# A transformer block pair on one Trainium2 core: order of work between the last attention step and the second MLP

## The chip, the cores and the metric

The kernel runs on one core of a Trainium2 chip. A core has a matrix engine (PE; its weight loads are listed apart as PEld), a vector engine (DVE), a scalar engine (ACT), a general engine (POOL) and a queue engine that issues transfers (SP). The engines run side by side and meet through semaphores. Matrix products land in PSUM, eight banks of 128 by 512 floats; everything else lies in on-chip SBUF or in HBM. The metric is the device time of the whole program in microseconds.

## The reference

The reference runs two layers over 256 latent tokens and 256 context tokens of width 1024. Layer 0 mixes by retention, layer 1 by neighbourhood attention with 32 heads; a squared-ReLU MLP of hidden width 4096 follows each. Six modulation vectors a layer come from a small product with `ada_w`. Only the latent tokens are returned, so layer 1 needs its MLP for 256 tokens alone. What matters here is the end of layer 1:

```python
x = layer_norm(DN_ALPHA * x + g1 * y, ln_g[i, 0], ln_b[i, 0])     # y = attention output @ nat_w_o
h = x * (1.0 + sc2) + sh2
x = layer_norm(DN_ALPHA * x + g2 * sq_relu_mlp(h, mlp_w1[i], mlp_w2[i]), ln_g[i, 1], ln_b[i, 1])

def sq_relu_mlp(h, w1, w2):
    return jnp.square(jax.nn.relu(h @ w1)) @ w2
```

All of it is float32. The kernel gets that from a faster format by splitting each operand into a high part, rounded to `float32r`, and a low part, the rest. A product is then three: high by high, high by low, low by high.

## The kernel before

**Weights.** `specs` lists all weight blocks in the order of use, each 512 KB. `fetch(n)` takes the next n: SP loads the block into one of four `raw` buffers, ACT casts it to a `hi` tile, and the subtraction that makes the `lo` tile is put on the list `pending`. `lows(n)` has DVE do the next n of that list. `take(n, ahead, open_)` hands out n blocks; first it fetches and subtracts until `ahead` blocks (five, where nothing is said) are there from its first on. There are five `hi` and five `lo` tiles. A `raw` buffer is free again once its low part is made, so SP's next load into it waits for DVE. With `at=` a block goes to a named slot (`hilo`), with `in_scratch` into small scratch tiles.

**Order.** Each engine has a queue that it works through in order. The wrappers `pe`, `act`, `dve` and `pool` have a switch `on`: while it is on, the engine keeps the order in which the program is written; while it is off, a scheduler chooses. In all that the change touches, the switch is on for PE, ACT and DVE (for POOL from line 1902 on); lines 2062 and 2063 turn it off inside the first feature block of the second MLP. SP always keeps the written order. So the written order is the order in each queue, and an instruction that waits holds back all behind it.

**The last attention step** (lines 1851 to 1872). Attention runs over 16 steps n. `scores(n)` multiplies queries and keys, `soften(n)` adds the bias and takes the exponential, `invert(n)` takes the reciprocal of the sums on DVE (and copies it to `rr`), `gather(n)` copies a corner of each result on POOL, `flip(n)` turns the results on PE (`ppt`) and copies them out (`pt`; the tiles j = 1 and 3 on DVE, the others on ACT), then turns `rr` into the bank `av`. `turned(n)` copies that to `rt`. `attend(n)` multiplies by the values, scales by `rt` on DVE and splits into `oTh` and `oTl`. Between them stand `fetch` and `lows` for the output weights.

**Output projection and norm** (lines 1874 to 2005). `mmo` multiplies `oTh` and `oTl` by output weights. `settle_last` and `settle_quarter` gate the result, add it to the residual `R`, and take statistics; `moments` ends with a power on POOL (`rstd`); `center` writes the normalised `xn`, half on DVE, half on ACT. `mod_pt` turns `xn` on PE, and `affine_half` (lines 1933 to 1939, token block 0) or `direct` (token block 1) scales, shifts and splits it into `hTh` and `hTl`.

**First feature block** (lines 2006 to 2048). Token blocks 0 and 1 become ready one after the other, so the first 512 features are done by tokens: `tok_part` multiplies one token block's `hTh` or `hTl` by a weight unit's high or low part. `p00`, `p01`, `p10` and `p11` are the banks for token block 0 or 1 and feature half 0 or 1 (all named `p1t` in the profile). HH is high by high, HL tokens high by weight low, LH tokens low by weight high. `activate` squares the ReLU on ACT and DVE (`r`), and `turn_block` turns the square on PE (`pt`) and splits it into `hid` on ACT and DVE.

**The other features** (lines 2054 to 2070). Seven blocks of two calls follow, by features: `mm1` does 48 products of 256 tokens into two banks `p`, and `relu_sq` squares and splits each. Then come the products with `mlp_w2`, gate, norm and output.

Of the kernel before, what the change touches and what calls it, by code (L numbers as in the profile page):

```python
# [10 lines left out]
F32 = mybir.dt.float32  # L11
# [98 lines left out]
def kernel(  # L110
# [23 lines left out]
    pe, act, dve, pool, sp = (  # L134
        InOrder(tc, getattr(nc, e), e in PIN)
        for e in ("tensor", "scalar", "vector", "gpsimd", "sync")
    )
# [19 lines left out]
    def nm(s):  # L157
        uid[0] += 1
        return f"{s}_{uid[0]}"
# [4 lines left out]
    def slot(i, shape, dt, s):  # L164

        return arena.tile(shape, dt, tag=f"s{i}", name=nm(s))

    def scr(s, dt=F32):
        return scp.tile([P, 512], dt, tag="scr", name=nm(s))
# [90 lines left out]
    def fetch(n, in_scratch=False, at=None):  # L260

        for src, k, ncol in specs[len(units) : len(units) + max(n, 0)]:
            raw = rawp.tile([P, k, ncol], F32, tag="raw", name=nm("raw"))
            sp.dma_start(out=raw[:], in_=src.rearrange("(k p) n -> p k n", p=P))
            if in_scratch or len(units) in scratch_units:
                hi, lo = Rows([scr("hi", F32R) for _ in range(k)]), Rows([scr("lo", F32R) for _ in range(k)])
                for i in range(k):
                    act.copy(out=hi[:, i, :], in_=raw[:, i, :])
                    pending.append((lo[:, i, :], raw[:, i, :], hi[:, i, :]))
                units.append((hi, lo))  # L270
                continue
            if at is None:
                hi = hip.tile([P, k, ncol], F32R, tag="hi", name=nm("hi"))
                lo = lop.tile([P, k, ncol], F32R, tag="lo", name=nm("lo"))
            else:
                both = slot(at, [P, 2, k, ncol], F32R, "hilo")
                hi, lo = both[:, 0], both[:, 1]
            act.copy(out=hi[:], in_=raw[:])
            pending.append((lo[:], raw[:], hi[:]))
            units.append((hi, lo))  # L280

    def lows(n=100):
        for lo, raw, hi in pending[:n]:
            dve.tensor_sub(out=lo, in0=raw, in1=hi.bitcast(F32))
        del pending[:n]

    def take(n, ahead=WB, open_=0):
        first = taken[0]
        while len(units) < min(first + max(n, ahead), len(specs)):
            fetch(1)  # L290
            lows()
        taken[0] = first + n
        assert len(units) - len(pending) >= first + n - open_
        return units[first : first + n]
# [312 lines left out]
    def mod_aff(pt, half, t, A, B, on_act=None, halves=False):  # L607

        tmp = scr("aff")
        for i in range(4):  # L610
            k = 4 * half + i
            a, b = A[:, k, t // 2 : t // 2 + 1], B[:, k, t // 2 : t // 2 + 1]
            o, x_ = tmp[:, tsl(i)], pt[:, tsl(i)]
            if halves:
                o = o.rearrange("p (b r c) -> p b r c", b=2, r=2)
                x_ = x_.rearrange("p (r b c) -> p b r c", b=2, r=2)
            if not (half if on_act is None else on_act):
                dve.tensor_scalar(out=o, in0=x_, scalar1=a, scalar2=b, op0=ALU.mult, op1=ALU.add)
            else:
                act.activation(out=o, in_=x_, func=AF.Identity, scale=a, bias=b)  # L620
        return tmp
# [40 lines left out]
    def rstd_of(mv, eng=pool):  # L662
        r = smp.tile([P, 1], F32, tag="rstd", name=nm("rstd"))
        eng.tensor_scalar_add(out=r[:], in0=mv[:, 1:2], scalar1=EPS)
        pool.tensor_tensor(out=r[:], in0=r[:], in1=mhalf[:], op=ALU.pow)
        return r
# [8 lines left out]
    def moments(t):  # L675
        mv = smp.tile([P, 2], F32, tag="mv", name=nm("mv"))
        dve.bn_aggr(out=mv[:], in_=stats[t][:])
        return mv, rstd_of(mv, dve)
# [38 lines left out]
    def add_to(t, half, tmp, eng):  # L717
        sl = slice(half * 512, (half + 1) * 512)
        eng.tensor_add(out=R[t][:, sl], in0=R[t][:, sl], in1=tmp[:])
# [120 lines left out]
    prs, pts, rows = {}, {}, {}  # L840
# [74 lines left out]
    def part_v(k, a, b):  # L915
# [8 lines left out]
        out=lgn[:, 0], in_=ret_decay[0].rearrange("(o d) h -> o (d h)", o=1).broadcast_to([P, 8])  # L924
# [121 lines left out]
    for h in range(RH):  # L1046
# [101 lines left out]
        for t in range(4):  # L1148
            po = bank("po")
            scs = list(range(4)) if t < 2 else [2, 3]  # L1150
            for i, sc in enumerate(scs):
# [9 lines left out]
                out=on, in0=po[:], scalar1=mv[:, 0:1], scalar2=r[:], op0=ALU.subtract, op1=ALU.mult  # L1161
# [36 lines left out]
        if not last:  # L1198
            for half in range(2):
                us = take(2)  # L1200
# [6 lines left out]
        else:  # L1207
# [17 lines left out]
            def turn(t):  # L1225
                return [mod_pt(xns[t], half) for half in range(2)]

            def affine(t, pts):
                return [mod_aff(pts[half], half, t, A, B) for half in range(2)]
# [64 lines left out]
    for hf in range(2):  # L1294
# [9 lines left out]
        if hf == 0:  # L1304
            us = take(2, 2)
# [4 lines left out]
            f2 = affine(2, turn(2))  # L1310
# [21 lines left out]
        for fp in range(len(hid), 8):  # L1332
            ht = hslot(fp)
            pb = [bank("p1") for _ in range(2)]
            us = take(2)
# [212 lines left out]
    sums, rrs, Es, pts, pss = {}, {}, {}, {}, {}  # L1548
# [37 lines left out]
    def av_half(n):  # L1586
        return av[0][:, 256 * (n % 2) : 256 * (n % 2) + 256]
# [48 lines left out]
    def turned(n):  # L1636

        rts[n] = smp.tile([P, P], F32, tag="rt", name=nm("rt"), bufs=2)
        act.copy(out=rts[n][:], in_=av_half(n)[:, P:])
# [92 lines left out]
    f2 = [mod_aff(p2[half], half, 2, A, B, True) for half in range(2)]  # L1732
# [128 lines left out]
    lows(1)  # L1861
    wo_first(1, 0)
    add_to(1, 0, t01[0], dve)
    lows(1)
    invert(n)
    gather(n)
    attend(n - 1)
    flip(n)
    turned(n)
    fetch(1, at=N_V)  # L1870
    lows(1)
    fetch(1, True)

    us = take(4, 0, 2)
# [55 lines left out]
    def toks(t):  # L1930
        return slice(AT + t * P, AT + (t + 1) * P)

    def affine_half(pts, half, t, on_act):
        aff = mod_aff(pts[half], half, t, A, B, on_act)
        ks = slice(4 * half, 4 * half + 4)
        hi, lo = hTh[:, ks, toks(t)], hTl[:, ks, toks(t)]
        av_ = aff[:].rearrange("p (k t) -> p k t", k=4)
        act.copy(out=hi, in_=av_)
        return lambda: dve.tensor_sub(out=lo, in0=av_, in1=hi.bitcast(F32))

    def direct(pts, t):

# [25 lines left out]
    def tok_part(ps, t, f2, a, b, ks=range(KC), start=False, stop=False):  # L1968
        for k in ks:
            pe.matmul(  # L1970
                ps[:, :256],
                lhsT=hs(k, toks(t).start, toks(t).stop)[a],
                rhs=us4[2 * f2 + k // 4][b][:, k % 4, :],
                start=start and k == ks[0],
                stop=stop and k == ks[-1],
            )

    def activate(ps):
        r = scr("r")[:, :256]
        act.activation(out=r, in_=ps[:, :256], func=AF.Relu)  # L1980
        dve.scalar_tensor_tensor(out=r, in0=ps[:, :256], scalar=0.0, in1=r, op0=ALU.max, op1=ALU.mult)
        return r

    def turn_block(r, t, f2, ht=ht):
        pt = bank("pt")
        for i in range(2):
            pe.transpose(pt[:, tsl(i)], r[:, tsl(i)], ident)
        src = pt[:, :256].rearrange("p (i t) -> p i t", i=2)
        hi, lo = (ht[:, 2 * f2 : 2 * f2 + 2, a, tsl(t)] for a in range(2))
        act.copy(out=hi, in_=src)  # L1990
        dve.tensor_sub(out=lo, in0=src, in1=hi.bitcast(F32))

    pts0 = [mod_pt(x0, half) for half in range(2)]
    lo0 = [affine_half(pts0, half, 0, True) for half in range(2)]
    ps = [wo_last(1, 1, cols) for cols in HALVES]
    for q in range(2):
        stat_quarter1(q)
# [3 lines left out]
    stats[1] = st1  # L2001
    fetch(2)
    us4 += take(2, 0, 2)
    mv1, r1 = moments(1)
    lo0[1]()
    p00, p01 = [bank("p1t") for _ in range(2)]
    LOW, HIGH = range(0, 4), range(4, KC)

    HH, HL, LH = (0, 0), (0, 1), (1, 0)
# [17 lines left out]
    p10, p11 = [bank("p1t") for _ in range(2)]  # L2027
# [4 lines left out]
    low1(0)  # L2032
    fetch(1)
    r00 = activate(p00)
    tok_part(p10, 1, 0, *LH, HIGH)
    tok_part(p11, 1, 1, *HH, start=True)
    tok_part(p11, 1, 1, *HL)
    tok_part(p10, 1, 0, *LH, LOW, stop=True)
    r01 = activate(p01)
    tok_part(p11, 1, 1, *LH, stop=True)  # L2040
    lows(1)
    fetch(1)
    turn_block(r00, 0, 0)
    turn_block(r01, 0, 1)
    r10 = activate(p10)
    lows(1)
    turn_block(r10, 1, 0)
    r11 = activate(p11)


    G2 = load_gate(1, 1, 1)
# [2 lines left out]
    for f4 in range(1, 8):  # L2054
        ht = slot(HS1[f4], [P, 4, 2, NLAT], F32R, "hid1")
        for f2 in range(2):
            us = take(2)
            pb = [bank("p1") for _ in range(2)]
            mm1(us, LAT, pb, at=AT)
            if f4 == 1 and f2 == 0:  # L2060
                turn_block(r11, 1, 1)
                for e in (pe, act, dve, pool):
                    e.on = False
            dve.on = f4 < 3
            for i in range(2):
                relu_sq(pb[i], LAT, ht[:, 2 * f2 + i, 0, :], ht[:, 2 * f2 + i, 1, :])
        hid.append(ht)
        if f4 in (1, 2):
            residual(f4 - 1, xn2[:, f4 - 1, :], gb, dve)
        dve.on = False  # L2070
# [125 lines left out]
```

## Time and profile before

| | us |
|---|---|
| three timed runs | 1211.16, 1213.59, 1215.23 |
| their median | 1213.59 |
| the profiled execution: span from first to last instruction | 1212.6 |
| PE busy | 1191.6 (98%) |
| DVE busy | 823.7 (68%) |
| ACT busy | 482.0 (40%) |
| POOL busy | 211.7 (17%) |
| DMA engines, mean rate | 160 GB/s |

For the profiled execution no time beside its span is given. In rows of groups or instructions, `hid<-pt` means that tile `hid` is written from `pt`; buffer numbers are left out, so many weight blocks share the names `raw`, `hi` and `lo`. Nearly all instructions carry line 89, that of the wrapper, so they are told apart by tiles. A timeline row gives start, duration, engine, operation, tiles, shape and count; the bracket at its end, where there is one, gives the idle time before it and what ended that. A row of waits gives who waited for whom, microseconds in total, how often, and the longest. A row of windows gives the length of the stretch, then busy time and count of PE, PEld, DVE, ACT and POOL (an engine may be absent if the question was narrowed to one tile), the granted clock of PE, the DMA engines' busy share and GB/s.

### The profile page before, as it was taken

What the parts mean: (1) busy time and instruction counts of PE and PEld (TensorE: products, weight loads), DVE (VectorE), ACT (ScalarE), POOL (GpSimd) and SP (SyncE); (2) the same over time, 40 slices, a digit from 0 to 9 for tenths busy, and PEclk for the clock granted to TensorE, in tenths of its full rate; (3) what the DMA queues carried; (4) which work ended last, traced back from release to release, by engine and by line L of the source; (5) the groups of instructions that cost most, each with busy time, mean ns of one, the idle gap of its engine ahead of it and who ended that gap; (6) DMA issues with size and microseconds to landing.
All of it is one profiled execution on the core that took longest, in us unless ns stands there. A gap on an engine that the chain in (4) does not pass through costs nothing.

```text
span 1212.6 us, 17987 instructions
## 1 busy us (share of the span) xinstructions
PE 1191.6 (98%) x6949; PEld 996.0 (82%) x6949; DVE 823.7 (68%) x1298; ACT 482.0 (40%) x809; POOL 211.7 (17%) x307
## 2 busy tenths in 40 slices
PE   7999999999999999999999999999999999999997
PEld 5777888888888889888888888889788878999886
DVE  3778857777685477667767675558576688777446
ACT  3562231323223146432123342227466566555341
POOL 1104501420340230000110000223344430000001
PEclk9999999999999999999999999999999999999999
DMA  9765443376543124326556566626244435566661
GB/s 301 228 221 200 139 132 109 115 257 138 136 141 122 57 70 142 111 95 203 185 189 228 180 217 208 208 83 202 82 140 124 121 124 155 172 202 194 228 207 40
DMA packets 147693, 194.29 MB, mean 160 GB/s; under 512 B 26960, under 2 KB 90760, under 8 KB 147608
## 3 DMA queue, kind: packets, MB, share of 16 engines
q1 hardware_dynamic: 141848, 181.08, 47.0%
q0 software_dynamic: 4608, 9.50, 2.8%
q10 hardware_dynamic: 1152, 2.57, 0.6%
q8 instruction: 54, 0.88, 0.3%
q14 instruction: 31, 0.25, 0.1%
HBM read 188.28 MB, written 5.75 MB: 160 GB/s over the span
## 4 chain that ended last, share of the span: by engine, by line
PE 88%; DVE 6%; ACT 3%; DMA 2%; issue 1%; POOL 1%; DVEq 0%; SPq 0%; ACTq 0%; POOLq 0%
PE p L89 42%; PE pq L89 7%; PE pv L89 7%; PE pw L89 6%; PE pg L89 6%; PE pn L89 5%; PE pnv L89 4%; PE pada L89 2%; PE po L89 2%; PE ppt L89 1%; PE pS L89 1%; PE pqk L89 1%; DMA rawa<-in_ada_w_dram 1%; DVE lo L89 1%; PE pav L89 1%
## 5 line engine op out<-in xcount | busy, mean ns | idle before, releaser
L89 DVE TENSOR_TENSOR lo<-raw,hi 128x1024 fp32r<-128x1024 f32 (+2 forms) x228 | 277.2, 1223 | 148.0 <-ACT hi L89 147.2
L89 ACT CAST hi<-raw 128x1024 fp32r<-128x1024 f32 (+2 forms) x228 | 233.6, 1033 | 355.1 <-PE p L89 187.8
L89 PE MATMUL p<-hi,hid 128*128 128x512 f32 (+1 forms) x832 | 242.4, 374 | 0.0
L89 PEld LDWEIGHTS p<-hi,hid 128*128 128x128 f32 x832 | 152.2, 188 | 28.9 <-issue 1.2
L89 PE MATMUL p<-hTh,hi 128*128 128x256 f32 (+1 forms) x512 | 169.7, 332 | 0.2 <-ACT hTh L89 0.2
L89 PE MATMUL p<-hTh,lo 128*128 128x256 f32 (+1 forms) x512 | 169.0, 330 | 0.8 <-DVE lo L89 0.8
L89 PE MATMUL p<-hTl,hi 128*128 128x256 f32 (+1 forms) x512 | 169.1, 330 | 0.4 <-DVE hTl L89 0.4
L89 PE MATMUL p<-lo,hid 128*128 128x512 f32 (+1 forms) x416 | 155.3, 373 | 0.0
L89 POOL TENSOR_TENSOR R<-R,acc 128x512 f32<-128x512 f32 x40 | 67.8, 1708 | 299.5 <-DVE acc L89 299.5
L89 PEld LDWEIGHTS p<-hTh,lo 128*128 128x128 f32 x512 | 98.1, 192 | 9.8 <-DVE lo L89 1.0
L89 PEld LDWEIGHTS p<-hTh,hi 128*128 128x128 f32 x512 | 97.0, 190 | 10.2 <-issue 1.2
L89 PEld LDWEIGHTS p<-hTl,hi 128*128 128x128 f32 x512 | 97.1, 190 | 9.3 <-DVE hTl L89 0.8
L89 DVE SCALAR_TENSOR_TENSOR acc<-rawa,scol,acc 128x1024 f32<-128x1024 f32 x56 | 71.1, 1281 | 32.8 <-DMA rawa<-in_ada_w_dram 32.7
L89 PEld LDWEIGHTS p<-lo,hid 128*128 128x128 f32 x416 | 78.4, 188 | 13.5
L89 DVE SCALAR_TENSOR_TENSOR strips<-rawa,scol,strips 128x512 f32<-128x512 f32 x84 | 70.2, 886 | 3.6 <-DMA rawa<-in_ada_w_dram 3.6
L89 POOL TENSOR_TENSOR rstd<-rstd,misc 128x1 f32<-128x1 f32 x28 | 19.1, 684 | 228.3 <-DVE rstd L89 226.3
L89 ACT CAST hid<-r 128x256 fp32r<-128x256 f32 (+1 forms) x64 | 32.0, 500 | 66.6 <-DVE r L89 66.3
L89 ACT ACTIVATE s<-s,mn 128x512 f32<-128x512 f32 x64 | 45.5, 712 | 26.2 <-DVE mn L89 26.2
L89 DVE TENSOR_TENSOR hid<-r,hid 128x256 fp32r<-128x256 f32 (+1 forms) x64 | 34.6, 541 | 26.7 <-ACT hid L89 26.6
L89 PE MATMUL pg<-hi,hTh 128*128 128x512 f32 x128 | 51.3, 401 | 0.0
L89 PE MATMUL pw<-hi,oh 128*128 128x512 f32 x128 | 51.2, 400 | 0.0
L89 PE MATMUL pw<-hi,ol 128*128 128x512 f32 x128 | 50.1, 391 | 0.5 <-DVE ol L89 0.5
(232 smaller groups left out, 2267.5 us busy)
## 6 DMA issues: line engine op xcount, KB each, us to landing
raw<-in_mlp_w_dram SPq DMA_DIRECT2D x128, 512.0 KB
rawa<-in_ada_w_dram SPq DMA_DIRECT2D x80, 512.0 KB
raw<-in_ret_w_in_dram SPq DMA_DIRECT2D x42, 512.0 KB
raw<-in_nat_w_in_dram SPq DMA_DIRECT2D x24, 512.0 KB
rawq<-in_ada_w_dram SPq DMA_DIRECT2D x16, 512.0 KB
raw<-in_ret_w_o_dram SPq DMA_DIRECT2D x16, 512.0 KB
bias<-rpb_rows POOLq DMA_DIRECT2D x32, 128.0 KB, 2.7
raw<-in_nat_w_o_dram SPq DMA_DIRECT2D x8, 512.0 KB
```

What stands on the lines that cost most here:

```text
L89: r = f(*args, **kwargs)
```

## The change

Five edits, all between the last attention step and the first `mm1` of the second MLP:

1. One `lows(1)` goes from ahead of `invert(n)` to behind `turned(n)`. It makes the low part of the second block of output weights.
2. `affine_half` takes an engine. Of the two low parts of token block 0, the second is subtracted on POOL in place of DVE; its call stands ahead of `moments(1)` in place of behind it.
3. In the products by tokens, `p11`'s HH products go ahead of `p10`'s LH products with the high half of the rows.
4. Only the squares of token block 0 are turned ahead of the first `mm1`; the two of token block 1 (`r10`, `r11`) are turned behind it. In the kernel before, `r10` was turned ahead of it, and `r11` behind it.
5. The second weight unit's low part is made ahead of the turns. `fetch(2)` and `lows(2)` behind the squares bring the next two units; the first `take` fetches none itself (`take(2, 0, 2)`), so the third unit's load, cast and subtraction come with the second `take`.

```diff
     add_to(1, 0, t01[0], dve)
-    lows(1)
     invert(n)
     gather(n)
     attend(n - 1)
     flip(n)
     turned(n)
+    lows(1)
     fetch(1, at=N_V)
...
-    def affine_half(pts, half, t, on_act):
+    def affine_half(pts, half, t, on_act, eng=dve):
...
-        return lambda: dve.tensor_sub(out=lo, in0=av_, in1=hi.bitcast(F32))
+        return lambda: eng.tensor_sub(out=lo, in0=av_, in1=hi.bitcast(F32))
...
-    lo0 = [affine_half(pts0, half, 0, True) for half in range(2)]
+    lo0 = [affine_half(pts0, half, 0, True, (dve, pool)[half]) for half in range(2)]
...
+    lo0[1]()
     mv1, r1 = moments(1)
-    lo0[1]()
...
     r00 = activate(p00)
+    tok_part(p11, 1, 1, *HH, start=True)
     tok_part(p10, 1, 0, *LH, HIGH)
-    tok_part(p11, 1, 1, *HH, start=True)
     tok_part(p11, 1, 1, *HL)
     tok_part(p10, 1, 0, *LH, LOW, stop=True)
     r01 = activate(p01)
     tok_part(p11, 1, 1, *LH, stop=True)
     lows(1)
     fetch(1)
+    lows(1)
     turn_block(r00, 0, 0)
     turn_block(r01, 0, 1)
     r10 = activate(p10)
-    lows(1)
-    turn_block(r10, 1, 0)
     r11 = activate(p11)
+    fetch(2)
+    lows(2)
...
-            us = take(2)
+            opening = f4 == 1 and f2 == 0
+            us = take(2, 0, 2) if opening else take(2)
             pb = [bank("p1") for _ in range(2)]
             mm1(us, LAT, pb, at=AT)
-            if f4 == 1 and f2 == 0:
+            if opening:
+                turn_block(r10, 1, 0)
                 turn_block(r11, 1, 1)
```

## The prediction

> **What bounds the kernel now.** I read the page's span first, then a table of ten-microsecond stretches, then TensorE's waits in the stretch of the change, and last the rows of each engine there. "This stretch" is 1000 to 1043 us: the last attention step, the output projection, the first feature block of the second MLP.
>
> ```profile
> span 1212.6 us, 17987 instructions
> ...
> 1030.00:1040.00 10.00, 7.88 (x56) 7.64 (x55) 8.39 (x14) 5.09 (x9) 0.00 (x0) 0.83 0.43 132
> ...
> 1042.80:1115.00 72.20, 72.20 (x616) 72.20 (x615) 55.53 (x84) 43.90 (x79) 0.00 (x0) 1.00 0.62 194
> ```
>
> The first figure after the length is PE's busy time, then come weight loads, DVE, ACT, POOL, and the granted clock. From 1042.8 PE never stands: 72.20 of 72.20 us. Before that it does, and in one stretch its clock is down too. So a microsecond that PE saves before 1043 us is a microsecond of the end, unless weights come late afterwards. Waits of PE, and one of its weight loads, in 1000 to 1043 us (total, count, longest):
>
> ```profile
> PE pt L89 <- DVE r L89: 2.1, 1, 2.1
> PE pav L89 <- DVE rt L89: 1.0, 1, 1.0
> ...
> PE pt L89 <- DVE xn L89: 0.4, 1, 0.4
> ...
> PEld pnw L89 <- ACT oTh L89: 0.5, 1, 0.5
> ```
>
> The first wait, and what follows it:
>
> ```profile
> 1032.60 0.60 PE L89 MATMUL pt<-cst,r 128*128 128x128 f32 x4
> 1035.32 0.44 PE L89 MATMUL pt<-cst,r 128*128 128x128 f32 x2 [2.12 <-DVE r L89]
> 1035.52 0.37 PE L89 MATMUL p<-hTh,hi 128*128 128x256 f32 x1
> ...
> 1042.81 0.36 PE L89 MATMUL p<-hTh,hi 128*128 128x256 f32 x1
> ...
> 1036.40:1039.85 3.45, 3.45 (x19) 3.45 (x18) 3.45 (x5) 0.99 (x2) 0.00 (x0) 0.51 0.55 162
> ```
>
> PE turns two squared blocks at 1032.60, stands until the third (r10) is squared, turns it, and only then starts the next 48 products. For 3.45 us of those its granted clock is 0.51.
>
> **The change, part by part.**
>
> *Low part of the last output weights, moved behind the last attention step's inverse and turn.* It is the subtraction at 999.59; the others are those that stand in DVE's queue around it, with the PE, SP and ACT rows that hang on it.
>
> ```profile
> 999.59 1.22 DVE L89 TENSOR_TENSOR lo<-raw,hi 128x1024 fp32r<-128x1024 f32 x1
> 1002.00 1.15 DVE L89 COPY pt<-ppt 128x384 f32<-128x384 f32 x2
> 1003.67 1.22 DVE L89 TENSOR_TENSOR hilo<-raw,hilo 128x1024 fp32r<-128x1024 f32 x1 [0.51 <-ACT hilo L89]
> 1004.81 0.28 DVE L89 TENSOR_TENSOR rt<-pav,rt 128x128 f32<-128x128 f32 x1
> ...
> 1001.49 0.33 PE L89 MATMUL pav<-cst,rr 128*128 128x128 f32 x1 [0.96 <-DVE rt L89]
> 1004.82 0.40 PE L89 MATMUL pnw<-lo,oTh 128*128 128x512 f32 x1
> ...
> 1000.88 0.38 SPq L89 DMA_DIRECT2D raw<-in_mlp_w_dram  x1
> ...
> 1014.29 1.03 ACT L89 CAST hi<-raw 128x1024 fp32r<-128x1024 f32 x1
> ```
>
> Inverse, `rr`, `rt`, `oTl` and both `pt` copies come 1.15 us sooner (the next DVE row starts 1.15 after 999.59), so PE's wait of 0.96 goes. But DVE has the same work before the `rt` at 1004.81: all that vanishes there is its idle 0.51 before `hilo`, because ACT also gets to that cast 1.15 sooner while DVE fills the time with the moved subtraction. `rt` is what the last products of the projection, then the statistics and everything after, wait for: gain 0.51, not 0.96. The products between now end sooner and PE stands longer ahead of them. The moved low part ends near 1003.2; its first user (1004.82) comes near 1003.6, so it is in time by 0.4. SP's load at 1000.88 waits for it (its buffer) and goes near 1003.3; the loads queued behind it go at 1004.92 or later, and ACT casts its data at 1014.29: free. Ends: 0.96 gained if `rt` did not stand behind `hilo`, 0.3 lost if the low part were 0.7 late.
>
> *One low part of token block 0 on Pool.* Rows of this place, then of two earlier places where Pool and DVE met.
>
> ```profile
> 1018.95 0.62 ACT L89 CAST hTh<-aff 128x512 fp32r<-128x512 f32 x1
> 1019.65 0.43 DVE L89 TENSOR_TENSOR R<-R,acc 128x256 f32<-128x256 f32 x1
> 1020.90 0.42 DVE L89 TENSOR_TENSOR R<-R,acc 128x256 f32<-128x256 f32 x1
> 1022.19 0.68 DVE L89 TENSOR_TENSOR hTl<-aff,hTh 128x512 fp32r<-128x512 f32 x1
> ...
> 1022.92 0.72 PE L89 MATMUL p1t<-hi,hTl 128*128 128x256 f32 x4 [0.19 <-DVE hTl L89]
> ...
> 1012.72 0.57 POOL L89 TENSOR_TENSOR rstd<-rstd,misc 128x1 f32<-128x1 f32 x1 [12.98 <-DVE rstd L89]
> 1022.35 0.92 POOL L89 TENSOR_TENSOR rstd<-rstd,misc 128x1 f32<-128x1 f32 x1 [9.07 <-DVE rstd L89]
> ...
> 448.53 1.40 DVE L89 TENSOR_TENSOR R<-R,acc 128x512 f32<-128x512 f32 x1
> 448.08 1.29 POOL L89 TENSOR_TENSOR hTl<-aff,hTh 128x512 fp32r<-128x512 f32 x1 [0.61 <-ACT hTh L89]
> ...
> 130.81 1.21 DVE L89 TENSOR_TENSOR lo<-raw,hi 128x1024 fp32r<-128x1024 f32 x1
> 130.64 2.61 POOL L89 TENSOR_TENSOR R<-R,acc 128x512 f32<-128x512 f32 x1 [2.29 <-DVE acc L89]
> ```
>
> The subtraction at 1022.19 costs DVE nothing (DVE then waits for Pool's `rstd`), but it slows `rstd` from 0.57 to 0.92: moving it gives 0.35 on the chain `rstd`, `xn`, next token block. Against that, Pool would take it at 1019.6 (cast ends 1019.57), 1.29 us long, across two DVE sums of `R`. Rows 448 and 130 show that these exclude each other: the sum started 0.45 after Pool took 1.40, twice that of its like; Pool, recorded 0.17 ahead of DVE, took 2.61, twice 1.29. Here DVE's first sum starts within 0.1 of Pool, so by the nearer row (130) DVE goes first; Pool then runs from 1020.08 to about 1021.3 and holds the second sum some 0.35 back. Net 0.0. Ends: 0.35 gained (no collision); 0.9 lost (Pool first: the sum of 1019.65 held to 1020.9, 1.25 later, less 0.35). Pool's next work, `rstd`, waits for nothing more; PE's user of this low part stands at 1022.92, behind Pool's end either way.
>
> [...]
>
> *High products of the next block first.*
>
> ```profile
> 1028.86 0.38 PE L89 MATMUL p1t<-hi,hTl 128*128 128x256 f32 x1 [0.30 <-DVE hTl L89]
> ...
> 1030.12 0.69 DVE L89 TENSOR_TENSOR hTl<-aff,hTh 128x512 fp32r<-128x512 f32 x1
> ```
>
> Eight products that need no low part (about 0.115 each) now fill this 0.30. The next low part (1030.12) ends at 1030.81, and PE gets to its users at about 1030.85: gain 0.30. Ends: 0 (that wait moves there) and 0.30.
>
> *The third and fourth squared block turned only behind the next 48 products.*
>
> ```profile
> 1031.39 1.22 DVE L89 TENSOR_TENSOR lo<-raw,hi 128x1024 fp32r<-128x1024 f32 x1
> 1034.85 0.41 DVE L89 SCALAR_TENSOR_TENSOR r<-p1t,r 128x256 f32<-128x256 f32 x1
> ...
> 1031.89 1.99 ACT L89 CAST hi<-raw 128x1024 fp32r<-128x1024 f32 x2 [1.21 <-PE p1t L89]
> 1034.31 0.39 ACT L89 ACTIVATE r<-p1t 128x256 f32<-128x256 f32 x1
> ...
> 1032.67 0.37 SPq L89 DMA_DIRECT2D raw<-in_mlp_w_dram  x1
> 1036.34 1.05 ACT L89 CAST hi<-raw 128x1024 fp32r<-128x1024 f32 x1
> ```
>
> r10's ReLU stood behind two weight casts on ACT, its square behind that on DVE. Now PE goes from the first two turns (four transposes, 0.2 a pair by 1035.32 to 1035.52, so to 1033.0) straight to the products: 1035.52 - 1033.0 = 2.52. One pair of transposes more is paid later, 0.2: net 2.32. Cover: the products need the low parts of both units. The first ends at 1032.6; the second, moved up behind it, near 1033.75, its user comes about 1034.6. In time by 0.9; if it were not, each microsecond late costs one.
>
> Two casts and two subtractions go behind r10 and r11, and the third load of the lookahead is taken one call later, with two more in one burst. The second 48 products would start near 1038.5 before the other gains; the two casts end near 1036 and the two low parts near 1037.3, free. The third products, 5.64 later, need a low part that now stands on DVE behind both turned blocks and the four-step chain (ReLU, square, cast, subtract) of two squares. A load takes up to 3.7 us from issue to use (1032.67 to 1036.34). Laid out with those durations the low part ends some 0.5 ahead of its user: free, but the thinnest cover of the change.
>
> *Clock.* The 48 products from 1035.52 to the next at 1042.81 took 7.29 with one pair of transposes (0.14); at the later pace (72.20 / 616 = 0.117) they take 5.64 and 0.14. So 1.5 us went to the 0.51 clock, right behind the 2.12 wait. With the wait gone I count the 1.5 as gained; the ends are 0 and 1.5.
>
> **Sum.** 0.51 + 0.0 + 0.30 + 2.32 + 1.5 = 4.6 us: 1212.6 becomes 1208.0. The profile gives no time beside its span; it lies 1.0 below the median of the three runs shown, 1213.59 (1211.16 to 1215.23). Laid on that: 1209.0, 0.38% less. About 0.3% (3.6 us) is what a measurement of this kernel can tell from no change.
>
> **The rivals.**
>
> *The half clock stays, or comes at another gap* (20%). For: the wait on ACT's `oTh` grows from 0.5 to about 0.9 near 1004, and the one on `xn` (0.4) stays. Against: neither is half of 2.12. The gain is 3.1: 1210.5, no difference. [...]
>
> *Pool goes first* (12%): 0.9 lost at `R`, gain 3.7: 1209.9, on the border; with a half clock behind the longer gap at 1024, 2.2.
>
> *Weights late for the third products* (6%), the slower case. DVE's first low part for them stands behind the squares; each of its steps waits for ACT, and ACT may stand before a cast for a load. If that ties up by L, PE stands L - 0.5 at about 1044. From L = 3.6 the idle brings back a half-clock stretch, 1.5, and the change is worth nothing (3.1 + 1.5 = 4.6); slower by 0.3% needs L of 7.2 (6.7 + 1.5 - 4.6), near two loads of 3.7 in a row: 1217.2. Against: behind 1042.8 the row of that stretch has the DMA engines busy for 0.62 of the time, so loads are not what is short.
>
> *More than summed* (7%): no collision, both waits of the first part gone: 0.8 more, 1208.2.
>
> **Numbers.** Forecast 1209.0, 55%: it, the last rival and half of the Pool case are over 0.3% faster; I take 0.62, 0.32 within, 0.06 slower, since 4.6 is only 1.0 above the bound. The likeliest case's own range is 1208 to 1210 (covers of 0.4 to 0.9 kept or just missed). The half-clock case with Pool first gives 1211.4, the runs of before spread 2 either way: 1207.0 to 1212.0.
>
> **What would show it.** Right: no wait of PE on `r` near 1033; clock 1.00 through 1030 to 1043; the `pav` wait gone, a wait on ACT's `oTh` of about 0.9 in its place; the first products on `p` about 3.3 sooner, the second about 4.6; Pool's `hTl` near 1.7 long; `rstd` 0.57. Wrong: a new wait of PE on `lo` in the third products, a stretch near clock 0.5 elsewhere, or a sum of `R` over 1 us.

## The result and the profile after

Run side by side, twelve times each, the kernel before took a median of 1213.38 us (1209.15 to 1216.22) and the changed kernel 1209.01 us (1207.65 to 1211.48). The ratio is 0.9972, with a 95% interval from 0.9961 to 0.9983: 3.4 us faster, at least 2.1 and at most 4.7. The forecast was 1209.0. The median met it, which is in part luck: the sum behind it, 4.6 us, was about one too large. The experiments below show that two of its steps failed, and that the pace of some products, which it did not have, moves a single execution by nearly as much as the whole change.

The page of the changed kernel, first line. The time of this execution was 1208.44 us.

```profile
span 1206.4 us, 17989 instructions
```

PE's waits in the changed kernel from 995 to 1060 us, and behind them one of its weight loads (total, count, longest):

```profile
PE pt L89 <- DVE xn L89: 0.6, 1, 0.6
PE pnw L89 <- ACT oTh L89: 0.6, 1, 0.6
PE p L89 <- DVE lo L89: 0.5, 1, 0.5
PE p1t L89 <- ACT hTh L89: 0.2, 1, 0.2
...
PEld pnw L89 <- ACT oTh L89: 1.0, 1, 1.0
```

The waits of 2.1 on `r` and 1.0 on `pav` are gone, as forecast. In place of the second, PE now waits 0.6 on `oTh`. The third row is new: PE stands for a low part, the sign that the prediction named for "wrong". Rows of PE in the changed kernel (start, duration):

```profile
1032.10 0.60 PE L89 MATMUL pt<-cst,r 128*128 128x128 f32 x4
1032.46 0.36 PE L89 MATMUL p<-hTh,hi 128*128 128x256 f32 x1
...
1038.20 0.60 PE L89 MATMUL pt<-cst,r 128*128 128x128 f32 x4
1038.55 0.37 PE L89 MATMUL p<-hTh,hi 128*128 128x256 f32 x1
...
1044.96 0.38 PE L89 MATMUL p<-hTh,lo 128*128 128x256 f32 x1 [0.48 <-DVE lo L89]
```

From the first turns to the products by features PE now needs 0.36 (1032.10 to 1032.46) where it needed 2.92; the 48 products and both late turns take 6.09 (1032.46 to 1038.55) where products and one turn took 7.29. The window that held the half clock, in the changed kernel:

```profile
1030.00:1040.00 10.00, 10.00 (x86) 9.85 (x85) 7.06 (x11) 6.34 (x11) 0.00 (x0) 1.00 0.62 191
```

PE is busy all through it, and the clock stands at 1.00.

**A ruler for all runs.** Five distances between rows that every kernel here has, in us, each from the start of one row to the start of the next: (1) from the last sum of `R` ahead of it to the last `rt`; (2) from there to `nmr` of the second half; (3) to the first turn of a square; (4) to the first product by features; (5) from there to the first product with `mlp_w2`. From that last point to the end it is 96.2 to 96.3 in every profile. The last column is the pace of the products by features at 1080 us, from start to start (see the pace, below).

| kernel | 1 | 2 | 3 | 4 | 5 | ns |
|---|---|---|---|---|---|---|
| before | 5.84 | 18.50 | 9.29 | 2.92 | 80.87 | 118 |
| before, second profile | 5.84 | 18.48 | 9.43 | 2.89 | 80.87 | 118 |
| before, third profile | 5.85 | 18.50 | 9.43 | 2.89 | 78.14 | 113 |
| changed | 5.22 | 18.33 | 9.08 | 0.35 | 77.68 | 113 |
| changed, second profile | 5.22 | 19.27 | 9.08 | 0.35 | 80.27 | 118 |
| first edit undone | 5.84 | 19.26 | 9.07 | 0.36 | 77.96 | 113 |
| second edit undone | 5.22 | 18.48 | 9.07 | 0.36 | 80.05 | 118 |
| third edit undone | 5.22 | 19.25 | 9.42 | 0.36 | 79.63 | 118 |
| fourth and fifth undone | 5.22 | 19.26 | 9.07 | 3.03 | 80.66 | 118 |
| fourth and fifth alone | 5.84 | 18.49 | 9.43 | 0.35 | 77.98 | 113 |
| low part behind the squares | 5.22 | 19.26 | 9.08 | 0.35 | 81.97 | 118 |
| third unit early | 5.22 | 19.27 | 9.08 | 0.35 | 76.94 | 113 |
| halves exchanged | 5.22 | 17.89 | 9.08 | 0.36 | 80.18 | 118 |
| both of these | 5.22 | 17.90 | 9.07 | 0.36 | 76.94 | 113 |

Columns 1 and 4 take only the values that an edit gives them, and column 3 does too but for its first row, which the pace explains. Column 2 and the pace do not: they differ between two profiles of one and the same kernel.

### The profile page after: what moved, and what is told of

Its sections match the earlier page's. It is cut to its first block, busy times and chain, and to the rows that moved or that the text cites. A ratio compares the mean times of both kernels' runs of the same rounds, so it can differ in the third digit from the quotient of the medians.

```text
span 1206.4 us, 17989 instructions
## 1 busy us (share of the span) xinstructions
PE 1187.1 (98%) x6949; PEld 992.0 (82%) x6949; DVE 822.0 (68%) x1297; ACT 480.7 (40%) x809; POOL 211.5 (18%) x308
## 4 chain that ended last, share of the span: by engine, by line
PE 86%; DVE 6%; ACT 3%; DMA 2%; issue 1%; POOL 1%; DVEq 0%; SPq 0%; ACTq 0%; POOLq 0%
PE p L89 41%; PE pq L89 7%; PE pv L89 7%; PE pw L89 6%; PE pg L89 6%; PE pn L89 5%; PE pnv L89 4%; PE pada L89 2%; PE po L89 2%; PE ppt L89 1%; DVE lo L89 1%; PE pS L89 1%; PE pqk L89 1%; DMA rawa<-in_ada_w_dram 1%; PE pav L89 1%
## 5 line engine op out<-in xcount | busy, mean ns | idle before, releaser
L89 PEld LDWEIGHTS p<-hTh,hi 128*128 128x128 f32 x512 | 96.3, 188 | 10.3 <-issue 1.2
L89 PE MATMUL pv<-hi,hTh 128*128 128x512 f32 x128 | 50.3, 402 | 0.0
```

Of the source, the lines that this page charges most:

```text
L89: r = f(*args, **kwargs)
```

## The experiments

The theory is the prediction's sum, edit by edit. Its rivals: Pool goes first; the half clock had another cause; waits only move. Times are ratios to the kernel before, which ran beside each group of kernels.

**Each edit undone.** Four kernels of one group.

```diff
     add_to(1, 0, t01[0], dve)
+    lows(1)
     invert(n)
...
     turned(n)
-    lows(1)
     fetch(1, at=N_V)
```

> The changed kernel with its first edit undone: the low part of the second output weight block stands ahead of the inverse again. Theory (the edit's 0.5 us were a true shortening of the way to rt): from the last sum of R to the rt scaling takes 5.8 us as in the kernel before, not 5.2; PE waits on rt for 0.9 again, the wait on oTh falls under 0.6; about 0.6 us slower than the changed kernel, near 1209.6. Rival (the wait only moved): the same time as the changed kernel within 0.2, because what rt gains is given back at the oTh wait or at the statistics behind it.

Measured: ratio 0.9968 (0.9956 to 0.9980). Distance 1 is 5.84 again, PE waits 0.9 on `rt`, and the wait on `oTh` is gone. So the edit is worth 0.62 up to `rt`. The rest of the way, 19.26, is as in the other kernels in which Pool goes first, so nothing of it is given back there. In whole times this can't be seen: the interval reaches 1.5 us to either side.

```diff
-    lo0 = [affine_half(pts0, half, 0, True, (dve, pool)[half]) for half in range(2)]
+    lo0 = [affine_half(pts0, half, 0, True, dve) for half in range(2)]
...
-    lo0[1]()
     mv1, r1 = moments(1)
+    lo0[1]()
```

> The changed kernel with its second edit undone: both low parts of token block 0 on DVE, the second behind the moments. Theory (a net of about nothing: 0.35 gained at rstd, 0.2 to 0.35 lost at the second sum of R): rstd takes 0.9 again, the sums of R 0.42 each, from rt to nmr as in the changed kernel within 0.2 us; same time within 0.2. [...]

Measured: ratio 0.9957 (0.9945 to 0.9969). Distance 2 is 18.48, as before the change. That is 0.15 more than in the first profile of the changed kernel, and 0.78 less than in the three others of this group, which have the edit. In these, Pool went first. The ratio is the best of the four, but the intervals of the first and the third kernel overlap it.

```diff
-    tok_part(p11, 1, 1, *HH, start=True)
     tok_part(p10, 1, 0, *LH, HIGH)
+    tok_part(p11, 1, 1, *HH, start=True)
```

> The changed kernel with its third edit undone: the high by high products of the second feature half stand behind the low by high ones again. Theory (the eight products fill a wait): PE stands 0.2 to 0.3 for the low part of token block 1 near 1028.5, 0.2 to 0.3 slower from nmr to the first turns. Rival (the wait moves to the next low part and back): no change of that stretch, no new wait.

Measured: ratio 0.9964 (0.9952 to 0.9977). PE stands 0.29 for `hTl` at 1028.37, and distance 3 is 9.42 in place of 9.08. The edit is worth 0.34.

```diff
-    lows(1)
     turn_block(r00, 0, 0)
     turn_block(r01, 0, 1)
     r10 = activate(p10)
+    lows(1)
+    turn_block(r10, 1, 0)
     r11 = activate(p11)
-    fetch(2)
-    lows(2)
...
-            us = take(2, 0, 2) if opening else take(2)
+            us = take(2)
...
-                turn_block(r10, 1, 0)
                 turn_block(r11, 1, 1)
```

> The changed kernel with its fourth and fifth edit undone: the third squared block is turned ahead of the first 48 products by features, the next weights come as before. Theory (the half clock follows the wait of about 2 us): PE stands about 2.1 us for r near 1032, then 3 to 3.5 us at a granted clock near 0.5; first products by features 2.5 us later than in the changed kernel, second products 3.7 later; 3.3 to 3.8 us slower, near 1212.5. Rival 1 (the half clock of the kernel before had another cause): the wait is there, the clock stays 1.00 or falls elsewhere, 2.3 slower. Rival 2 (the wait given back in later stretches): under 1 us slower. The new wait of PE on a low part in the third products goes in every case, which is 0.5 the other way.

Measured: ratio 0.9989 (0.9980 to 0.9997), the one kernel of the group that loses most of the gain. Two of PE's waits (the first is back, the second is Pool's doing), and the window of its half clock:

```profile
PE pt L89 <- DVE r L89: 2.1, 1, 2.1
PE pt L89 <- DVE xn L89: 1.7, 1, 1.7
```

```profile
1034.56:1037.97 3.41, 3.35 (x16) 3.36 (x17) 3.35 (x6) 1.59 (x3) 0.00 (x0) 0.50 0.49 135
```

Counted from the first turns, the second products by features come 3.66 us later than in the first profile of the changed kernel (10.11 for 6.45), as the theory had it. With the wait on `r` the half clock is back too. The wait of 1.7 in the same trace, ten microseconds earlier, left the clock at 1.00.

**The changed kernel once more.** No edit; the question is what differs between two executions.

> The changed kernel itself, profiled once more. Three things differed between profiles so far without a difference in the code there: which of Pool's low part and DVE's sum of R goes first (DVE in the first profile of the changed kernel: 18.3 us from rt to nmr; Pool in three of its relatives: 19.3), and the pace of the products by features (113 or 118 ns each, held from one stop of PE to the next). Theory (both are settled anew in each execution, by less than the trace resolves): the way from rt to nmr is 18.3 or 19.3 and nothing between, and the pace is 113 or 118 and nothing between; if Pool goes first a sum of R takes 1.58 in place of 0.43. Rival (they are properties of the program): 18.3, 113 ns and a sum of R of 0.43 again. Time near 1209 to 1211.

Measured: ratio 0.9969 (0.9958 to 0.9981). Distance 2 is 19.27, the pace 118 ns: both differ from the first profile, so neither is a property of the program. Pool and the first sum of `R` of the last 512 columns, in the first profile of the changed kernel:

```profile
1019.55 1.59 POOL L89 TENSOR_TENSOR hTl<-aff,hTh 128x512 fp32r<-128x512 f32 x1 [6.37 <-ACT hTh L89]
...
1019.55 0.43 DVE L89 TENSOR_TENSOR R<-R,acc 128x256 f32<-128x256 f32 x1
1020.79 0.63 DVE L89 TENSOR_TENSOR R<-R,acc 128x256 f32<-128x256 f32 x1
```

and in the second:

```profile
1018.92 1.31 POOL L89 TENSOR_TENSOR hTl<-aff,hTh 128x512 fp32r<-128x512 f32 x1 [6.36 <-ACT hTh L89]
...
1018.94 1.57 DVE L89 TENSOR_TENSOR R<-R,acc 128x256 f32<-128x256 f32 x1
1021.33 0.43 DVE L89 TENSOR_TENSOR R<-R,acc 128x256 f32<-128x256 f32 x1
...
1022.79 0.55 POOL L89 TENSOR_TENSOR rstd<-rstd,misc 128x1 f32<-128x1 f32 x1 [2.56 <-DVE rstd L89]
```

In the first, both start in the same hundredth, DVE's sum takes its usual 0.43 and Pool 0.3 more than its 1.3. In the second, Pool starts 0.02 ahead, and the sum takes 1.57. Seven profiles here have this edit: in six Pool starts ahead by 0.01 to 0.02 and the sum takes 1.57 or 1.58; only in the one shown first it does not. The edit's price is then 19.27 less 18.50: it loses 0.77. The sum is held 1.15, and `rstd`, 0.55 for 0.92, gives 0.37 of that back. Where DVE wins, the edit gains 0.17.

**The third unit early.**

```diff
-    fetch(2)
-    lows(2)
+    fetch(3)
+    lows(3)
```

> The changed kernel with three units in place of two fetched and subtracted behind the squares, so that the low part for the third products stands ahead of the late squares on DVE. Theory of waits: PE's wait of 0.48 on a low part at 1045 goes, nothing else changes, 0.3 to 0.5 us faster than the changed kernel. Rival (theory of the pace): in all four profiles the products after that wait ran at 113 ns, and in three of the four those before it at 118; with the wait gone the 118 ns hold to the end of the products by features, 576 times 4.5 ns is 2.6 us, less 0.5: some 2 us slower than the changed kernel in an execution that starts with 118.

What the wait at 1044.96 hung on in the changed kernel: two loads and a window of the time that they took, then ACT, then DVE:

```profile
1032.39 0.37 SPq L89 DMA_DIRECT2D raw<-in_mlp_w_dram  x1
...
1033.49 0.37 SPq L89 DMA_DIRECT2D raw<-in_mlp_w_dram  x1
...
1034.00:1039.00 5.00, 5.00 (x45) 5.00 (x45) 3.06 (x5) 3.08 (x5) 0.00 (x0) 1.00 0.90 281
```

```profile
1036.11 1.06 ACT L89 CAST hi<-raw 128x1024 fp32r<-128x1024 f32 x1 [0.16 <-DMA raw<-in_mlp_w_dram]
1038.93 1.05 ACT L89 CAST hi<-raw 128x1024 fp32r<-128x1024 f32 x1 [1.76 <-DMA raw<-in_mlp_w_dram]
1039.88 0.37 ACT L89 ACTIVATE r<-p 128x256 f32<-128x256 f32 x1
1040.16 0.64 ACT L89 CAST hid<-pt 128x256 fp32r<-128x256 f32 x2
```

```profile
1040.55 0.76 DVE L89 TENSOR_TENSOR hid<-pt,hid 128x256 fp32r<-128x256 f32 x2 [3.49 <-ACT hid L89]
...
1043.69 3.49 DVE L89 TENSOR_TENSOR lo<-raw,hi 128x1024 fp32r<-128x1024 f32 x3
```

PE turns the late squares at 1038.20, but ACT casts them only at 1040.16: it stood 1.76 ahead of a weight cast for a load. By the order of loads and casts it is the load of 1033.49, which went 1.10 behind another: the one was used 3.72 after its issue (1036.11), the other 5.44 after (1038.93), and in that time the DMA engines were busy for 0.90. DVE idles 3.49 for the squares' cast at 1040.16 and has the squares and only then the low part, which ends near 1044.9. With the third unit early, DVE:

```profile
1037.70 1.23 DVE L89 TENSOR_TENSOR lo<-raw,hi 128x1024 fp32r<-128x1024 f32 x1 [0.20 <-ACT hi L89]
1040.99 0.76 DVE L89 TENSOR_TENSOR hid<-pt,hid 128x256 fp32r<-128x256 f32 x2 [2.06 <-ACT hid L89]
```

The low part stands in what was idle time, and the trace shows no wait of PE from 1025 to the products with `mlp_w2`. Ratio 0.9972 (0.9958 to 0.9985): no difference from the changed kernel in the same group. The 0.5 is less than the interval resolves, so its worth in whole time is not shown. The rival was not put to the test: in this execution the products went from 118 to 113 ns already behind the late turns, at 1039.

**The halves exchanged.** The first low part of token block 0 goes on Pool, the second on DVE.

```diff
-    lo0 = [affine_half(pts0, half, 0, True, (dve, pool)[half]) for half in range(2)]
+    lo0 = [affine_half(pts0, half, 0, True, (pool, dve)[half]) for half in range(2)]
...
-    lo0[1]()
     mv1, r1 = moments(1)
+    lo0[1]()
```

> The changed kernel with the halves exchanged: the first low part of token block 0 on Pool, the second on DVE behind the moments as in the kernel before. Theory (Pool would take the port at 1017.4, 0.3 behind DVE's start on a sum of R and long before the next one, so nothing is decided by a few ns; DVE loses 0.68 of work ahead of the last two sums of R): both sums of R take 0.43, rstd 0.9, from rt to nmr 17.9 us (18.5 with both low parts on DVE, less 0.6): 0.4 faster than the changed kernel where DVE went first, 1.3 faster than where Pool did. Rival (Pool holds a sum of R anyway, or PE's products for the next columns end it): 18.5 or more, no gain over both on DVE.

Pool, then the three sums of `R`, in this kernel:

```profile
1017.54 1.49 POOL L89 TENSOR_TENSOR hTl<-aff,hTh 128x512 fp32r<-128x512 f32 x1 [4.30 <-ACT hTh L89]
...
1017.17 0.69 DVE L89 TENSOR_TENSOR R<-R,acc 128x512 f32<-128x512 f32 x1
1019.01 0.42 DVE L89 TENSOR_TENSOR R<-R,acc 128x256 f32<-128x256 f32 x1
1020.25 0.43 DVE L89 TENSOR_TENSOR R<-R,acc 128x256 f32<-128x256 f32 x1
```

DVE is on its sum 0.37 ahead of Pool, Pool is through at 1019.03, as the next sum starts, and none of the sums is held. Distance 2 is 17.89, as forecast (17.9): 1.38 less than where Pool goes first. Ratio 0.9962 (0.9951 to 0.9973), 0.8 us better than the changed kernel beside it, which the intervals do not separate; the profiled execution drew 118 ns.

**The second unit's low part behind the squares.** A wait of PE at another place.

```diff
-    lows(1)
     turn_block(r00, 0, 0)
     turn_block(r01, 0, 1)
     r10 = activate(p10)
     r11 = activate(p11)
+    lows(1)
     fetch(2)
```

> The changed kernel with the second unit's low part behind the two late squares, the rest as it is. PE starts the 48 products, does the first 12 (1.4 us) on the first unit and then stands for that low part, by the rows of DVE until about 1035.9, so some 2.0 us. Theory (a half clock of 3.4 us follows any wait of about 2 us): the granted clock falls to 0.50 within a microsecond or two of that wait's end, and the second products come 3.5 us later than in the changed kernel. Rival (1.6 us of waiting at 1023 left the clock at 1.00 in three profiles, so the length alone does not do it): the clock stays 1.00, 2.0 later. By the cover that the prediction gave this step, 0.9, the wait should be no less than 1.5.

PE's waits on `lo` (two: this one and the one in the third products), its row, and a window that holds it:

```profile
PE p L89 <- DVE lo L89: 2.0, 2, 1.2
```

```profile
1036.30 0.39 PE L89 MATMUL p<-hTh,lo 128*128 128x256 f32 x1 [1.18 <-DVE lo L89]
```

```profile
1034.00:1040.00 6.00, 4.82 (x41) 4.62 (x40) 4.51 (x7) 3.70 (x6) 0.00 (x0) 1.00 0.68 200
```

Ratio 0.9975 (0.9963 to 0.9988). The wait is 1.18, not 2.0, mainly for two reasons: the first two products of a unit need only its high part, which the expectation left out, and the low part, which ends near 1036.2, comes 3.0 behind the first of the products (1033.23) where the expectation had 3.4. The clock stays at 1.00. What was meant as the test of a wait of about 2 shows only that one of 1.18, at this place, left the clock as it was.

**The fourth and fifth edit alone**, on the kernel before (the reverse of the diff above).

> The kernel before with the fourth and fifth edit alone. By the stages measured so far the other three come to nothing (0.62 gained before rt, 0.2 to 0.3 before the first turns, 0.8 lost between where Pool goes first). Theory (these two edits carry the whole change): the third turns and the second products come 3.7 us sooner, counted from the first turns, PE stands 0.3 to 0.5 for a low part at 1045, the ratio to the kernel before is that of the changed kernel, 0.997. Rival (the other three add what was summed for them, 0.8): a ratio nearer 0.998. A sum of R takes 0.43, rstd 0.9.

Measured: ratio 0.9976 (0.9964 to 0.9988). From the first turns to the second products it takes 6.45 (1032.17 to 1038.62); in the kernel before it took 10.21 (1032.60 to 1042.81). That is 3.76 sooner. PE waits 0.37 on `lo` at 1044.93. By these distances the two edits carry the change; the whole times can't tell theory and rival apart, for both, 0.8 us from each other, are inside the interval.

**Both improvements at once**: third unit early and halves exchanged.

> The changed kernel with the halves of token block 0 exchanged (first low part on Pool) and three units fetched behind the squares: both single changes at once. Theory: 17.9 us from rt to nmr (as with the exchange alone), no wait of PE on a low part near 1045 (as with the third unit alone): 1.0 faster than the exchange alone is not to be had from the second, only its 0.25 to 0.5; against the changed kernel 1.4 and 0.5 in a usual execution, so some 1.5 to 2 faster, near 1208, ratio to the kernel before 0.995 to 0.996. Rival (the pace hides it: the medians of executions move with the share that draws 113 or 118 ns, 2.6 us apart): no difference from the changed kernel that the interval resolves.

Measured: median 1206.92 us, ratio 0.9948 (0.9934 to 0.9962), by it 6.3 us faster than the kernel before, about what the theory gave. PE's waits from 1000 to 1115 us:

```profile
PE pnw L89 <- ACT oTh L89: 0.6, 1, 0.6
PE pt L89 <- DVE xn L89: 0.3, 1, 0.3
```

No other wait of PE there is longer than 0.15. The ruler gives 1.37 at distance 2 and the 0.5 of the wait on `lo` against a usual execution of the changed kernel, 1.9; the ratios (0.9948 here, 0.9972 and 0.9969 there) give 2.5 to 2.9, but the two were not run side by side, the intervals overlap a little, and this kernel's one profile drew 113 ns.

**The kernel before, twice more.** No edit.

> The kernel before, profiled once more, for the half clock. Its record comes in windows of 3.41 us. Twice the clock was halved in the window that followed one with 2.0 to 2.1 us of PE standing in it; six times a wait of 1.6 left it at 1.00. Theory (what counts is the standing inside one window, with a threshold between 1.66 and 2.03): PE stands 2.1 us for r near 1033; if the edges of the windows (counted in steps of 3.413 from the end of the first stretch of clock) leave at least 2.0 of it in one, the next window has 0.50; if an edge leaves no more than 1.6 in either, the clock stays 1.00 and the 48 products take 5.7 us in place of 7.1. Rival (the length of the wait alone): 0.50 in either case.

> The same kernel and question as the run before it, with another position of the windows. Theory and rival as there: 0.50 where a window holds at least 2.0 us of the wait, 1.00 where none holds more than 1.6; by the rival 0.50 always.

The half clock, in the second profile and then in the third:

```profile
1036.46:1039.87 3.41, 3.41 (x19) 3.41 (x18) 3.41 (x6) 1.42 (x3) 0.00 (x0) 0.50 0.51 147
```

```profile
1035.35:1038.77 3.42, 3.42 (x19) 3.42 (x18) 3.42 (x6) 1.55 (x3) 0.00 (x0) 0.50 0.43 138
```

Both waits were 2.10, from 1033.60 and from 1032.74. The window ahead of the half clock, 3.41 long, reaches from 1033.05 in the one and from 1031.94 in the other: either holds the whole wait. So the two rules were not told apart; a wait cut by an edge did not occur.

## The pace of the products by features

These two profiles of one kernel took 1215.0 and 1211.46 us. Their rulers differ by more than 0.02 in column 5 alone, by 2.73, and ahead of it the third profile is 0.88 earlier (its last sum of `R` starts at 998.37, the other's at 999.25). Windows of 40 us in them, second profile, then third:

```profile
1060.00:1100.00 40.00, 40.00 (x342) 40.00 (x341) 30.52 (x47) 24.03 (x44) 0.00 (x0) 1.00 0.68 208
```

```profile
1060.00:1100.00 40.00, 40.00 (x355) 40.00 (x354) 31.12 (x48) 23.71 (x45) 0.00 (x0) 1.00 0.66 205
```

Both are full, at a granted clock of 1.00, and yet one holds 342 matmuls and the other 355. Row by row, second profile, then third:

```profile
1060.11 0.28 PE L89 MATMUL p<-hTh,lo 128*128 128x256 f32 x1
1060.23 0.28 PE L89 MATMUL p<-hTh,hi 128*128 128x256 f32 x1
1060.35 0.28 PE L89 MATMUL p<-hTl,hi 128*128 128x256 f32 x1
1060.46 0.28 PE L89 MATMUL p<-hTh,lo 128*128 128x256 f32 x1
```

```profile
1060.13 0.28 PE L89 MATMUL p<-hTh,hi 128*128 128x256 f32 x1
1060.24 0.28 PE L89 MATMUL p<-hTl,hi 128*128 128x256 f32 x1
1060.35 0.28 PE L89 MATMUL p<-hTh,lo 128*128 128x256 f32 x1
1060.47 0.28 PE L89 MATMUL p<-hTh,hi 128*128 128x256 f32 x1
```

In the one, products start every 118 ns (0.35 for three), in the other every 113 (0.34). At 1080 us all fourteen profiles have one or the other, eight the slower and six the faster (the ruler's last column). In the first profile of the kernel before, the pace was 118 ns up to the stop of 0.30 for a low part at 1028.86 and 113 behind it, 113 behind the half clock's end at 1039.87, and 118 behind the late turn at 1042.67, for some 620 products, to 1116.39. In the first profile of the changed kernel it was 118 up to the late turns at 1038.20 and 113 behind them, and still 113 behind the stop of 0.48 at 1044.96, to 1110.14. Over the 620 products behind the late turns, 4.5 ns make 2.8 us, against 3.4 for the whole change. What makes the two paces, and which one follows a stop, was not settled: the same wait in the changed kernel was followed by 113 ns in one profile and 118 in the other.

## Why the prediction was right, and where it was not

**First edit: right, 0.62 for 0.51.** `rt` comes sooner by more than DVE's idle 0.51: rows of DVE that follow without a stop start some 0.1 ahead of the recorded end of the one before (1004.81, where 1003.67 and 1.22 make 1004.89), and the idle time had cost that overlap too. In the row that the prediction read, that of the weight load, the wait on `oTh` grew from 0.5 to 1.0, forecast 0.9; PE itself waits 0.56.

**Second edit: wrong in the usual execution.** The step that failed is "by the nearer row (130) DVE goes first". Here the two starts lie 0.02 us apart at most, and in six of seven profiles Pool is ahead, by 0.01 to 0.02: 0.77 lost, near the 0.9 that the prediction gave as its end. Row 130 showed the opposite with Pool recorded 0.17 ahead (DVE 1.21, Pool 2.61), and so does the changed kernel's profile (DVE 1.20 from 131.24, Pool 2.61 from 131.07); why is open. But the profile of the kernel before had a nearer row, which the prediction did not use:

```profile
591.34 1.30 POOL L89 TENSOR_TENSOR R<-R,acc 128x512 f32<-128x512 f32 x1
591.34 2.38 DVE L89 TENSOR_TENSOR lo<-raw,hi 128x1024 fp32r<-128x1024 f32 x1
```

Both start in the same hundredth, Pool takes its usual 1.30, and DVE 2.38 in place of 1.22; the changed kernel's profile has the same two durations, both from 591.80. So a tie should have had the rival at no less than half, not 12%, and a sum of `R` over 1 us, one of the prediction's signs for "wrong", is what six of seven profiles show. Where DVE did go first, the second sum was held 0.21 and the sum of the step is a gain of 0.17, forecast 0.0.

That Pool would take a "port", as the expectation for the exchanged halves has it, no run shows. What the rows show is which of two operations took longer than its like: 1.57 for 0.43, 2.38 for 1.22, and Pool's own 2.61 for 1.29.

**Third edit: right, 0.35 for 0.30** (9.43 to 9.08). The first profile showed less, 9.29, because some 30 products behind that wait drew 113 ns.

**Fourth and fifth edit: right.** Distance 4 falls from 2.89 to 0.35, 2.54, forecast 2.52; four transposes later take 0.35 where two took 0.14, 0.21, forecast 0.2. The second unit's low part was in time.

**"The thinnest cover": wrong by one microsecond.** The low part for the third products was to end 0.5 ahead of its user and came 0.5 late (0.48 and 0.54 in the two profiles). What the layout had too small is a load's time: 3.7 from issue to use, as one load alone had taken, where the second of two close ones took 5.44. So ACT stood 1.76 ahead of the cast at 1038.93, behind which the casts of the turned squares queue. That this stand made PE's wait is read from the rows; no run shortened the load. It is the mechanism of the slower rival, with low parts 1.0 later than laid out where a slower kernel needed 7.2. Its counter-argument, DMA engines busy for 0.62, was a mean over 72 us; in the 5 us that counted they were busy for 0.90.

**Clock: right, 1.4 for 1.5.** The 48 products took 7.15 (7.29 less one turn) and take 5.74 (1032.46 to 1038.20). The half clock came in four of four profiles with the wait of 2.1 and in none of the ten without it (between the program's first and last 20 us), so the 1.4 belongs to the fourth and fifth edit. That the wait itself brings the half clock is not shown by a run of its own: the one that was to make such a wait elsewhere made one of 1.18.

**The sum** for a usual execution is 0.62 - 0.77 + 0.35 + 2.54 - 0.21 + 1.41 - 0.5 = 3.4, against 4.6 forecast; the ratio gives 3.4 on the shared runs and 3.8 on those of the second group. The ruler's five columns for the two second profiles, both at 118 ns, add up to 117.51 and 114.19: 3.3. The forecast's 1209.0 laid 4.6 on a median of three, 1213.59; by the ratio that is 1210.2. That the median of the changed kernel came out at 1209.01 is luck, and may owe something to the pace that its executions drew; only two of its executions have a profile, which shows the pace.

## What to carry to other kernels

Where an operation of one engine is held by another's, as a sum of `R` was here by Pool's low part (1.57 for 0.43, with starts 0.01 to 0.02 apart), do not let the two start that close: put the operation where the other is clearly under way, as the exchanged halves do (DVE 0.37 ahead, no sum held), and count a tie as lost. When weight low parts queue behind work that needs another engine, follow that engine's queue to its loads before calling a cover kept, and do not give two loads in a row the time that one took alone (5.44 for the second, 3.7 for one alone). Profile a kernel more than once before laying a gain of a few microseconds to an edit: take the distances between rows, and leave out the stretches whose pace changes without a cause in the code (here 113 or 118 ns).

## What was not expected of the hardware

The two paces are the first: 113 or 118 ns for the same product of 256 columns at a granted clock of 1.00 (355 and 342 matmuls in the 40 us of two profiles of one kernel). In the two first profiles a change came at a stop of 0.30 and at late turns, and none at a stop of 0.48.

The half clock is the second: in the four profiles that have it, it lasted 3.41 us, and it followed windows in which PE stood for 2.03 to 2.13 us of the 3.41, about six tenths. All stretches of the clock's record inside the program were whole multiples of 3.413 in both first profiles (1020.59, 299 of them, then 1 and 49 in the kernel before; 347 in the changed one). Waits of 1.60 to 1.66 (six profiles; the longest lay whole in one window) and 1.18 left the clock at 1.00. What a wait between 1.66 and 2.03 does was not measured.
